# Experts of at most 64 tokens with their high and low parts side by side, in pairs, and weights split 2048 columns at a time

## The chip, the core and the metric

One core of a Trainium2 chip. A time is the device time of one execution of the whole program, in microseconds (us). Beside the times there is a profile of one execution, with a record for each instruction of the engines: TensorE (PE, with its weight loads, PEld), VectorE (DVE), ScalarE (ACT), GpSimd (POOL), and of the queues that issue DMAs (SPq is the sync engine's).

## What is computed

One decoder layer on 512 tokens of 1024 values. Its first part (norms, two kinds of attention, an output projection) is not touched. The second part is a mixture of 32 experts, of which each token takes four:

```python
logits = jnp.dot(xf, w_router) + b_router            # top 4 of 32, softmax over the four
def expert_block(args):
    xb, eb = args
    up = jnp.dot(xb, w_up[eb]) + b_up[eb]            # 1024 x 2048
    glu, lin = jnp.split(up, 2, axis=-1)
    glu = jnp.minimum(glu, 7.0)
    lin = jnp.clip(lin, -7.0, 7.0)
    act = glu * jax.nn.sigmoid(1.702 * glu) * (lin + 1.0)
    return jnp.dot(act, w_down[eb]) + b_down[eb]     # 1024 x 1024
```

The output of a token is the sum of its four experts' rows, weighted with the softmax, then normed and added to the token. With these inputs the 30 experts that are sorted by their tokens (experts 0 and 1 are not) have 169, 122, 118, 112, 107, 106, 99, 81, 80, 78, 77, 75, 71, 70, 63, 62 and then 54 to 13 tokens.

## The kernel before

All values are float32. To multiply them at nearly that precision, an operand is split into a high part (rounded to the matmul's fp32r, on ScalarE) and a low part (the rest, on VectorE); a product is then high by high, high by low and low by high, three matmuls that add up in PSUM.

The tokens of one expert are gathered into slots, on partitions. A step handles 128 slots (or 256). KINDS names the 21 steps: nine S (one expert, 128 slots), eight T (two experts, 96 and 32 slots), three P (two experts, 64 slots each) and one X (one expert, 256 slots); experts with many tokens are put, by a rank that the program works out, where there are many slots. For each expert w_up is read in eight blocks of 128 x 2048 and w_down in four of 256 rows, which also are 128 x 2048 in memory: twelve weights of 1.05 MB each. The loads go through the sync engine's queue into NW = 10 raw buffers (rawtile), each issued as its buffer comes free. wsplit (L1089) makes high and low parts, in two halves of 1024 columns each, out of NH = 8 and NL = 5 buffers; both instructions are recorded at L111. mm_w (L1128) multiplies: the slots' transposed activations are the stationary operand, the weight is the moving one, 512 columns at a time. Each block of 512 columns takes three matmuls: high x by high w (L1131), high x by low w (L1132), low x by high w (L1134). In steps T and P the second expert goes first, over all slots up to its end, and the first one then starts its slots anew, so that both share the PSUM tiles ug, ul (up) and dn (down); a matmul has 64, 96 or 128 stationary columns. A bias is added by a matmul of the rows bt with a column of ones (mm_b, L1140).

In a step the order of the listing is: up of this step's experts, two weights of the previous step's down split ahead (NA), the transposes of the next step's tokens (tsplit, L1119), the activation (act_part, L1163: two clips on VectorE, a sigmoid on ScalarE, a product on GpSimd at L1167, a last product on VectorE), then the previous step's down, its copy out of PSUM (ScalarE, L1226) and its scatter to memory (GpSimd's queue, L1217), and the transposes of the activation. The listing's order isn't the order on an engine: a planner with a cost model of its own chooses, ahead of the run, in which order each engine issues what is ready by the model; each engine then keeps that order and waits where it must.

The last expert's result goes into the sum over each token's rows without a scatter (from L1464 on). After it stands a loop for tokens past their expert's slots (from L1504 on), which has nothing to do with these counts, in either form of the kernel.

Of the kernel before, what the change touches and what calls it, by code (L numbers as in the profile page):

```python
# [9 lines left out]
F32 = mybir.dt.float32  # L10
# [20 lines left out]
NW = 10  # L31
NH = 8
NL = 5

# The slots of the experts of a step: S and X one expert, the others several that share 128. The first E0 steps take
# experts 0 ... E0 - 1; the others go by the number of tokens, those with most to the places with most slots. Tokens past
# the slots of an expert are left to a loop at the end.
SLOTS = {"S": (128,), "X": (256,), "P": (64, 64), "T": (96, 32)}
KINDS = "SSTTPSTPXTTSSSSTPTTSS"
# [3 lines left out]
def _steps():  # L43
    """(slots, first place) of the steps, the rank by tokens that each place takes, and the slots by rank"""
# [9 lines left out]
C_ID, C_IO, C_E, C_R, C_P0, C_J, C_KY, C_KP, C_K = 0, 128, 256, 288, 320, 321, 325, 357, 358   # kept to the end  # L54
C_TI, C_TS, C_NM, C_VR, C_N = 0, 128, 256, 384, 385                         # up to the experts
# [51 lines left out]
    # hi (ACT) and lo (DVE) float32r parts of src  # L107
# [11 lines left out]
def emit(tc, A, dbg=None, stop_at=99):  # L119
# [57 lines left out]
    # silu(c)  # L177
# [6 lines left out]
    strip = dram.tile([8, 128, 384], F32, name="strip")      # the biases of distances 255 ... -128, 128 times  # L184
    far = k.sp.tile([128, 8], F32, name="far")               # the bias of all larger distances
# [11 lines left out]
    def ada(part):  # L197
# [12 lines left out]
        # column (j, b) of this part is 32 * j of block b  # L210
# [5 lines left out]
    def rstd_of(ss, n, name):  # L216
        """1 / sqrt(ss / n + eps): a first guess from the exponent, then two steps of third order."""
# [20 lines left out]
    def rstd_ln(ss, n, name):  # L238
        """the same from ln and exp, with a Newton step."""
# [1317 lines left out]
```

## Time and profile before

| | us |
|---|---|
| median of three runs | 1755.59 |
| least and greatest of them | 1754.2, 1759.06 |
| profiled execution, first to last instruction | 1753.6 |
| TensorE busy in it | 1634.2 |
| VectorE busy | 1409.0 |
| ScalarE busy | 1085.6 |
| GpSimd busy | 202.9 |

The profiled execution's span is 2 us under the median. A matmul's end is modelled in the trace, and successive ones overlap: its pace is read from the starts. The share of busy time is an average over a first part of some 449 us, the experts, and the end.

### The profile page before, as it was taken

To read this page: it belongs to the slowest core of one execution; us is meant where nothing else is said; L and a number is where in the kernel's file an instruction comes from. 1 tells how busy PE (TensorE), PEld (TensorE's weight loads), DVE (VectorE), ACT (ScalarE), POOL (GpSimd) and SP (SyncE) were. 2 spreads that over 40 slices of the span, in tenths; PEclk is the share of its full clock that TensorE was granted. 3 is DMA by queue.
4 is the path that set the end of the run, shared out by engine and by line. 5 is a ranking of instruction groups with operands and counts; after the bars stand their busy time and mean duration, and the time that the engine had idled before them with its cause. 6 is when DMAs were issued, how large, how long until landed. Compare 5 with 4: busy or idle time off the path is not lost.

```text
span 1753.6 us, 22917 instructions
## 1 busy us (share of the span) xinstructions
PE 1634.2 (93%) x7691; PEld 1205.0 (69%) x7691; DVE 1409.0 (80%) x1848; ACT 1085.6 (62%) x1373; POOL 202.9 (12%) x180
## 2 busy tenths in 40 slices
PE   6999999987799999999999999999999999999980
PEld 2878765766577777777767777777777767677760
DVE  2885657768898898897985887899997888888877
ACT  3554445654667777766665666777776668576741
POOL 0200201003510110010101101011110100000002
PEclk9999999996799999999999999999999999999995
DMA  8522264085779899898886798899899989898842
GB/s 280 158 72 73 82 249 175 25 281 236 267 296 365 341 339 398 344 344 346 327 323 251 293 360 295 324 354 365 336 357 369 350 316 371 304 361 321 329 192 111
DMA packets 120575, 494.42 MB, mean 282 GB/s; under 512 B 13658, under 2 KB 38723, under 8 KB 84739
## 3 DMA queue, kind: packets, MB, share of 16 engines
q1 hardware_dynamic: 112723, 472.12, 71.5%
q0 software_dynamic: 7728, 20.77, 3.5%
q8 instruction: 62, 1.02, 0.2%
q14 instruction: 62, 0.51, 0.1%
HBM read 473.45 MB, written 25.69 MB: 285 GB/s over the span
## 4 chain that ended last, share of the span: by engine, by line
PE 61%; DVE 6%; issue 1%; DMA 1%; ACT 1%; POOL 0%; DVEq 0%; ACTq 0%
PE ug L1131 6%; PE dn L1132 6%; PE ul L1131 6%; PE ug L1132 6%; PE ul L1132 6%; PE dn L1131 6%; PE ul L1134 6%; PE ug L1134 6%; PE dn L1134 6%; DVE wlo L111 3%; PE aT L1119 1%; PE dn L1140 1%; PE ug L1140 1%; DMA raw<-in_w_up_dram 1%; PE xT L1119 1%
## 5 line engine op out<-in xcount | busy, mean ns | idle before, releaser
L111 DVE TENSOR_TENSOR wlo<-raw,whi 128x1024 fp32r<-128x1024 f32 x768 | 922.8, 1251 | 101.2 <-ACT whi L111 54.9
L111 ACT ACTIVATE whi<-raw 128x1024 fp32r<-128x1024 f32 x768 | 771.7, 1053 | 235.4 <-PE ug L1134 126.9
L1132 PE MATMUL dn<-wlo,ah 128*128 128x512 f32 (+2 forms) x528 | 211.9, 401 | 12.5 <-DVE wlo L111 12.5
L1131 PE MATMUL dn<-whi,ah 128*128 128x512 f32 (+2 forms) x528 | 212.2, 402 | 3.9 <-ACT ah L111 3.9
L1131 PE MATMUL ug<-whi,xh 128*128 128x512 f32 (+2 forms) x496 | 199.3, 402 | 4.5 <-DVE g L1164 2.2
L1131 PE MATMUL ul<-whi,xh 128*128 128x512 f32 (+2 forms) x496 | 198.4, 400 | 1.8 <-ACT whi L111 1.8
L1132 PE MATMUL ug<-wlo,xh 128*128 128x512 f32 (+2 forms) x496 | 197.2, 398 | 0.1
L1132 PE MATMUL ul<-wlo,xh 128*128 128x512 f32 (+2 forms) x496 | 196.5, 396 | 0.0
L1134 PE MATMUL dn<-whi,al 128*128 128x512 f32 (+2 forms) x528 | 167.9, 398 | 0.0
L1134 PE MATMUL ug<-whi,xl 128*128 128x512 f32 (+2 forms) x496 | 156.9, 395 | 0.0
L1134 PE MATMUL ul<-whi,xl 128*128 128x512 f32 (+2 forms) x496 | 155.5, 395 | 0.0
L1167 POOL TENSOR_TENSOR l<-l,g 128x1024 f32<-128x1024 f32 (+1 forms) x22 | 64.7, 2941 | 666.8 <-DVE l L1165 499.0
L1132 PEld LDWEIGHTS dn<-wlo,ah 128*128 128x128 f32 (+2 forms) x528 | 94.0, 178 | 44.9 <-DVE wlo L111 17.7
L1131 PEld LDWEIGHTS dn<-whi,ah 128*128 128x128 f32 (+2 forms) x528 | 94.0, 178 | 37.1 <-issue 6.7
L1131 PEld LDWEIGHTS ug<-whi,xh 128*128 128x128 f32 (+2 forms) x496 | 87.7, 177 | 37.1 <-issue 5.4
L1134 PEld LDWEIGHTS dn<-whi,al 128*128 128x128 f32 (+2 forms) x528 | 93.2, 178 | 28.5
L1131 PEld LDWEIGHTS ul<-whi,xh 128*128 128x128 f32 (+2 forms) x496 | 87.6, 177 | 30.4 <-ACT whi L111 4.5
L1132 PEld LDWEIGHTS ul<-wlo,xh 128*128 128x128 f32 (+2 forms) x496 | 87.4, 176 | 29.9 <-issue 1.9
L1132 PEld LDWEIGHTS ug<-wlo,xh 128*128 128x128 f32 (+2 forms) x496 | 87.8, 177 | 27.6 <-DVE wlo L111 2.0
L1134 PEld LDWEIGHTS ug<-whi,xl 128*128 128x128 f32 (+2 forms) x496 | 87.5, 177 | 28.0 <-DVE xl L111 0.4
L1134 PEld LDWEIGHTS ul<-whi,xl 128*128 128x128 f32 (+2 forms) x496 | 87.3, 176 | 27.8
L1217 POOL DMA_INDIRECT y<-g,dis x22 | 28.2, 1280 | 284.3 <-ACT g L1226 283.9
(520 smaller groups left out, 2345.7 us busy)
## 6 DMA issues: line engine op xcount, KB each, us to landing
raw<-in_w_up_dram SPq DMA_DIRECT2D x247, 1024.0 KB, 6.9
raw<-in_w_down_dram SPq DMA_DIRECT2D x128, 1024.0 KB, 7.3
wada<-in_w_ada_dram SPq DMA_DIRECT2D x24, 1024.0 KB, 6.7
y<-zero SPq DMA_DIRECT2D x4, 2048.0 KB, 14.3
raw<-in_w_up_dram SPq DMA_DIRECT2D x16, 512.0 KB, 6.8
raw<-y SPq DMA_DIRECT2D x7, 1024.0 KB, 9.0
wor<-in_w_out_dram SPq DMA_DIRECT2D x4, 1024.0 KB, 5.5
x<-in_x_dram SPq DMA_DIRECT2D x8, 256.0 KB, 5.8
```

Of the source, the lines that this page charges most:

```text
L111: return (nc.scalar.activation(hi, src, AF.Copy), nc.vector.tensor_sub(lo, src, hi.bitcast(F32)))
L1119: nc.tensor.transpose(pz[:, kk, :], src[:, kk * 128:(kk + 1) * 128], ident)
L1131: nc.tensor.matmul(o[0:r], lhsT=xT[0][:, kk, 0:r], rhs=wh, start=first, stop=False)
L1132: nc.tensor.matmul(o[0:r], lhsT=xT[0][:, kk, 0:r], rhs=wl, start=False, stop=False)
L1134: nc.tensor.matmul(o[0:r], lhsT=xT[1][:, kk, 0:r], rhs=wh, start=False, stop=False)
L1140: nc.tensor.matmul(o[0:r], lhsT=sel_[h].to_broadcast([64, r]), rhs=bt[h, c:c + 512], start=False, stop=True)
L1167: nc.gpsimd.tensor_tensor(l, l, g, op=OP.mult)
L1217: st = nc.gpsimd.indirect_dma_start(out=y4, out_offset=bass.IndirectOffsetOnAxis(ap=di, axis=0), in_=ys, in_offset=None, bounds_check=S * ...
```

## The change

- KINDS has 24 steps: fifteen S, one X and eight H. H has two experts of at most 64 tokens. tsplit puts, for each expert of an H, the high parts of its 64 slots and then the low parts next to each other, so that 128 stationary columns hold both. mm_w then takes two matmuls for each 512 columns (that operand by high w, and by low w) instead of three; PSUM partitions 0 to 63 hold the products of the high parts, 64 to 127 those of the low parts. T and P are gone.
- To add the two halves of an H, mm_c copies partitions 64 to 127 of PSUM into bt (ScalarE, two copies of 1024 columns for up, one for down), and a matmul with cm (the bias selector above an identity, written by GpSimd for each pair) adds them and the bias to partitions 0 to 63. Each expert of an H has an activation (act_part) and a copy out of its own, on 64 partitions; the last product (act_end) and the scatter are common to the pair.
- wsplit splits 2048 columns with one instruction on each engine, with three buffers of 2048 for the high and three for the low parts; the raw buffers are nine.
- The activation has no product on GpSimd: VectorE clips and multiplies in one instruction that reads PSUM, and clips the sigmoid with the last product.
- up and down are generators that the loop interleaves: an H's two ups each with a piece of the previous step's down behind it; after an H, each half of an S's up is followed by the down of one of the two experts.
- In mm_w the order of the matmuls of other steps is high by high, low by high, high by low. Bias rows lie in a [128, 3072] tile on 64 partitions for all columns.

The core of the diff:

```diff
-NW = 10
-NH = 8
-NL = 5
+NW = 9
+NH = 3
+NL = 3
+SG7 = 1.0 / (1.0 + math.exp(-1.702 * 7.0))
-SLOTS = {"S": (128,), "X": (256,), "P": (64, 64), "T": (96, 32)}
-KINDS = "SSTTPSTPXTTSSSSTPTTSS"
+SLOTS = {"S": (128,), "X": (256,), "H": (64, 64)}
+KINDS = "SSHHXHSSHSSHSSSHSSSHSSHS"
...
     def wsplit(raw):
-        for h in range(2):
-            hi, lo = (wp.tile([128, 1024], F32R, name=f"w{t}{h}{nb[0]}", tag=t, bufs=n) for t, n in (("hi", NH), ("lo", NL)))
-            k.split(hi, lo, f[:, h * 1024:(h + 1) * 1024])
+        hi, lo = (wp.tile([128, 2048], F32R, name=f"w{t}{nb[0]}", tag=t, bufs=n) for t, n in (("hi", NH), ("lo", NL)))
+        k.split(hi, lo, f)
...
     tsplit:
+        t = ep.tile([128, 8, 256], F32R, name=f"{nm}t{nb[0]}", tag=f"t{s_}")
+        w = kd[0] if len(kd) > 1 else 128
+        v = t.rearrange("p k (e c s) -> p (k e) c s", c=2, s=w)
+        return t, k.split(v[:, :, 0], v[:, :, 1], pz.rearrange("p k (e s) -> p (k e) s", s=w)), s_
...
+    def mm_w(outs, xT, kk, ws, first, j=None, last=False):
+        if j is not None:
+            x = xT[0][:, kk, 128 * j:128 * j + 128]
+            for c in range(2):
+                for o, w in zip(outs, ws):
+                    nc.tensor.matmul(o, lhsT=x, rhs=w[c], start=first and c == 0, stop=last and c == 1)
+            return
...
+    def mm_c(ps_, cm, c0):
+        for n, pt in enumerate(ps_):
+            nc.scalar.activation(bt[64:128, c0 + 1024 * n:c0 + 1024 * n + 1024], pt[64:128].rearrange("p a n -> p (a n)"),
+                                 AF.Copy)
+        for n, pt in enumerate(ps_):
+            for h in range(2):
+                c = c0 + 1024 * n + 512 * h
+                nc.tensor.matmul(pt[0:64, h], lhsT=cm, rhs=bt[:, c:c + 512], start=False, stop=True, skip_group_check=True)
...
-    def act_part(pg_, pl_, g, l, sg, mid=None):
-        nc.vector.tensor_scalar(g, pg_, 7.0, None, op0=OP.min)
+    def act_part(pg_, pl_, l, sg):
         nc.vector.tensor_scalar(l, pl_, 8.0, -6.0, op0=OP.min, op1=OP.max)
-        nc.scalar.activation(sg, g, AF.Sigmoid, scale=1.702)
-        nc.gpsimd.tensor_tensor(l, l, g, op=OP.mult)
-        if mid:
-            mid()
-        nc.vector.tensor_tensor(l, l, sg, op=OP.mult)
+        nc.scalar.activation(sg, pg_, AF.Sigmoid, scale=1.702)
+        nc.vector.scalar_tensor_tensor(l, pg_, 7.0, l, op0=OP.min, op1=OP.mult)
+    def act_end(l, sg):
+        nc.vector.scalar_tensor_tensor(l, sg, SG7, l, op0=OP.min, op1=OP.mult)
...
     down_gen, after the last of four weights:
+        for py in pys:
+            if j is None:
+                mm_b([py[:, 0], py[:, 1]], sel_, (2048, 2560))
+            else:
+                mm_c((py,), sel_, 2048)
...
     the loop over the steps:
+        if pair:
+            nc.gpsimd.tensor_copy(cm[0:64], sel[:, 1, e:e + 2][:, :, None].to_broadcast([64, 2, 64]))
+                ups = [(up_gen(xT, wus[j], sel_[j], lambda pg_, pl_, o=slice(64 * j, 64 * j + 64): act_part(
+                    pg_[0:64], pl_[0:64], l[0][o], sg[o]), j), 8) for j in range(2)]
+            dns = [(0, 4), (1, 4)] if pn == "H" else [(0, 4)] if pn == "X" or len(ups) == 1 else [(0, 2), (0, 2)]
+        if len(ups) < len(dns):
+            ups = [(ups[0][0], 4), (ups[0][0], 4)]
+        for n, (g_, c) in enumerate(ups):
+            for _ in range(c):
+                fin = next(g_)
+            if n < len(dns):
+                pd.ahead(dns[n][0], NA)
...
+            if fin:
+                fin()
+            if last and not two:
+                act_end(l[0], sg)
+            if n < len(dns):
+                pd.run(*dns[n])
```

## Rows read from the trace of the kernel before

**Rows 1.** The busy time of each stretch (columns: stretch, its length, then busy us and instruction count of PE, weight loads, DVE, ACT, POOL, then granted TensorE clock, share of the DMA engines and GB/s): all that lies ahead of the experts, the experts' weights, and the end.

```profile
0.00:449.30 449.30, 398.27 (x2211) 299.31 (x2212) 299.05 (x787) 221.13 (x500) 52.85 (x100) 0.94 0.48 165
449.30:1676.00 1226.70, 1204.81 (x5355) 883.28 (x5356) 1049.67 (x980) 838.69 (x844) 134.32 (x73) 0.99 0.88 333
...
1686.00:1753.60 67.60, 22.72 (x89) 15.98 (x87) 50.29 (x76) 19.54 (x24) 12.43 (x6) 0.70 0.42 167
```

**Rows 2.** The waits of the experts' stage: TensorE's longest, the loads' queue (SPq) and ScalarE's (who waited for whom, us in total, times, longest).

```profile
PE dn L1132 <- DVE wlo L111: 10.8, 8, 1.6
...
SPq L945 <- DVE wlo L111: 521.6, 192, 9.8
...
ACT whi L111 <- PE ug L1134: 126.9, 159, 2.1
```

**Rows 3.** The page's groups of matmuls (line, engine, operation, output<-operands, shapes, count, busy us and mean ns, idle before); each output has as many in L1132 and in L1134, and ul has as many as ug.

```profile
L1131 PE MATMUL dn<-whi,ah 128*128 128x512 f32 (+2 forms) x528 | 212.2, 402 | 3.9 <-ACT ah L111 3.9
L1131 PE MATMUL ug<-whi,xh 128*128 128x512 f32 (+2 forms) x496 | 199.3, 402 | 4.5 <-DVE g L1164 2.2
...
L1131 PE MATMUL u<-whi,xh 128*128 128x512 f32 x64 | 25.5, 399 | 0.5 <-DVE sg L1165 0.4
```

**Rows 4.** The timeline of TensorE at the start of two weights that follow each other in the fifth step, whose experts have 64 slots (twelve matmuls lie between the starts), and at the step's transposes (start, us, engine, line, operation).

```profile
702.98 0.40 PE L1131 MATMUL ug<-whi,xh 128*64 128x512 f32 x1
...
705.75 0.40 PE L1131 MATMUL ug<-whi,xh 128*64 128x512 f32 x1
...
709.45 1.09 PE L1119 MATMUL xT<-cst,xg 128*128 128x128 f32 x8
```

**Rows 5.** The timeline of GpSimd, only its product of each step's activation (L1167): its starts mark the steps. The second step (511.55), two steps T (1049.33, 1122.18), three steps S (1223.07 to 1297.78), the last step.

```profile
511.55 2.37 POOL L1167 TENSOR_TENSOR l<-l,g 128x1024 f32<-128x1024 f32 x1 [22.75 <-DVE l L1165]
...
1049.33 2.77 POOL L1167 TENSOR_TENSOR l<-l,g 128x1024 f32<-128x1024 f32 x1 [47.95 <-DVE tis L1072]
...
1122.18 2.42 POOL L1167 TENSOR_TENSOR l<-l,g 128x1024 f32<-128x1024 f32 x1 [42.91 <-DVE l L1165]
...
1223.07 3.33 POOL L1167 TENSOR_TENSOR l<-l,g 128x1024 f32<-128x1024 f32 x1 [23.28 <-DVE l L1165]
...
1259.99 3.33 POOL L1167 TENSOR_TENSOR l<-l,g 128x1024 f32<-128x1024 f32 x1 [23.49 <-DVE tis L1072]
...
1297.78 3.32 POOL L1167 TENSOR_TENSOR l<-l,g 128x1024 f32<-128x1024 f32 x1 [21.06 <-DVE l L1165]
...
1678.90 3.30 POOL L1167 TENSOR_TENSOR l<-l,g 128x1024 f32<-128x1024 f32 x1 [26.16 <-DVE l L1165]
```

**Rows 6.** Groups of VectorE and ScalarE over the whole span, by shape, and one piece of VectorE's timeline in the sixth step.

```profile
L111 DVE TENSOR_TENSOR wlo<-raw,whi 128x1024 fp32r<-128x1024 f32 x768 | 922.8, 1251 | 101.2 <-ACT whi L111 54.9 <-PE ug L1132 13.3 <-PE u L1132 12.3
...
L1164 DVE TENSOR_SCALAR g<-ug 128x1024 f32<-128x1024 f32 x20 | 24.5, 1223 | 20.7 <-PE ul L1140 19.9
...
L111 DVE TENSOR_TENSOR wol<-wor,woh 128x2048 fp32r<-128x2048 f32 x4 | 9.2, 2289 | 4.0 <-ACT woh L111 4.0
...
L111 ACT ACTIVATE whi<-raw 128x1024 fp32r<-128x1024 f32 x768 | 771.7, 1053 | 235.4 <-PE ug L1134 126.9 <-PE dn L1134 57.8 <-PE u L1134 15.5
...
L111 ACT ACTIVATE woh<-wor 128x2048 fp32r<-128x2048 f32 x4 | 7.7, 1913 | 0.7 <-PE y L95 0.5
...
719.66 9.35 DVE L111 TENSOR_TENSOR wlo<-raw,whi 128x1024 fp32r<-128x1024 f32 x8
```

**Rows 7.** VectorE's split at the time of GpSimd's product: the timeline of the last step, and the tile's durations (ns: least, median, longest).

```profile
1678.73 4.56 DVE L111 TENSOR_TENSOR wlo<-raw,whi 128x1024 fp32r<-128x1024 f32 x2
...
L111 DVE TENSOR_TENSOR wlo<-raw,whi x768: 1203/1218/3470, 441.8 to 1699.5; 128x1024 fp32r<-128x1024 f32 x192
```

**Rows 8.** Windows of the experts' stage in which the DMA engines' share was 0.99 to 1.00 (columns as in rows 1), and the page's line of the software queue, which holds the gathers and scatters.

```profile
659.00:684.00 25.00, 25.00 (x112) 19.52 (x111) 21.82 (x21) 18.49 (x19) 1.02 (x1) 1.00 1.00 409
684.00:709.00 25.00, 25.00 (x110) 14.49 (x109) 20.69 (x18) 17.10 (x18) 0.00 (x0) 1.00 1.00 379
...
1010.00:1020.00 10.00, 10.00 (x46) 8.19 (x45) 8.85 (x8) 7.05 (x8) 0.00 (x0) 1.00 0.99 351
...
q0 software_dynamic: 7728, 20.77, 3.5%
```

**Rows 9.** The end of a step on the timeline: the fifth step's last bias products, ScalarE's copy of the result and the next weight's first product; and the same at the last step.

```profile
733.69 0.70 PE L1140 MATMUL dn<-bt,sel 64*96 64x512 f32 x2
...
734.48 1.02 ACT L1226 ACTIVATE g<-dn 128x1024 f32<-128x1024 f32 x1 [1.01 <-PE dn L1140]
735.17 0.48 PE L1131 MATMUL ug<-whi,xh 128*128 128x512 f32 x1
...
1689.24 1.02 ACT L1226 ACTIVATE g<-dn 128x1024 f32<-128x1024 f32 x1 [7.05 <-PE dn L1140]
...
1691.23 0.50 PE L1131 MATMUL dn<-whi,ah 128*128 128x512 f32 x1 [1.79 <-ACT ah L111]
```

**Rows 10.** Windows around the start of the experts (columns as in rows 1), and TensorE's timeline in the first of them.

```profile
430.00:440.00 10.00, 0.92 (x19) 0.64 (x18) 9.71 (x37) 1.55 (x3) 2.50 (x2) 0.50 0.57 211
...
449.87 0.63 PE L1132 MATMUL ug<-wlo,xh 128*128 128x512 f32 x1
450.29 0.63 PE L1131 MATMUL ug<-whi,xh 128*128 128x512 f32 x1
```

More of the change, by code (lines that the diff above doesn't have):

```diff
@@ L1149, in up, with up_gen @@
+    def up_gen(xT, wsrc, sel_, act_, j=None, gate=(), between=iter(())):
         pg_, pl_ = ptile("ug", "uA"), ptile("ul", "uB")
         outs = [pg_[:, 0], pg_[:, 1], pl_[:, 0], pl_[:, 1]]
[L1151 to L1159 removed]
@@ L1390, in emit @@
         sel_ = [sel[:, int(i >= E0), x:x + 1] for x in range(e, e + len(ws_))]
-        two = kd[0] > 128
+        two, pair = kd[0] > 128, len(kd) > 1
+        if pair:
+            cm = cmb[nh % 2]
+            nh += 1
+            nc.gpsimd.tensor_copy(cm[0:64], sel[:, 1, e:e + 2][:, :, None].to_broadcast([64, 2, 64]))
+            sel_ = [cm[:, j] for j in range(2)]
         xs = [gather(ti) for ti, _ in idx[i + 1]] if i + 1 < len(steps) else []
+        kn = steps[i + 1][0] if i + 1 < len(steps) else ()
@@ L1393, in emit @@
         if two:
-            pu = up_act2(xT, wus[0], sel_)
-        elif i == 0:
-            pu = up(xT, kd, wus, sel_, (first,) + xT[2], between)
-            rank, xi, pos2, tab2 = tb
-        else:
-            pu = up(xT, kd, wus, sel_)
-        if i == 1:
-            prev = (tsplit(l[0], "a"),), *prev[1:]
-        if i + 1 >= E0 and (i + 1 - E0) % NB == 0 and i + 2 < len(steps):
-            prep(range(i + 2, min(i + 2 + NB, len(steps))))
-        if i == XS + 3:
-            selx, xrow = more(rank, xi)
@@ L1406, in emit @@
[L1406 to L1414 removed]
+            l = [etile("l"), etile("sg")]
+            g_ = up2_gen(xT, wus[0], sel_[0], l)
+            ups = [(g_, 4), (g_, 4)]
+        else:
+            l, sg = [etile("l")], etile("sg")
+            if pair:
+                ups = [(up_gen(xT, wus[j], sel_[j], lambda pg_, pl_, o=slice(64 * j, 64 * j + 64): act_part(
+                    pg_[0:64], pl_[0:64], l[0][o], sg[o]), j), 8) for j in range(2)]
+            else:
+                ups = [(up_gen(xT, wus[0], sel_[0], lambda pg_, pl_: act_part(pg_, pl_, l[0], sg),
+                               gate=((first,) + xT[1]) if i == 0 else (), between=between if i == 0 else iter(())), 8)]
@@ L1415, in emit @@
+        aTs = [tsplit(a, "a", kd) for a in l]
         if len(xs) > 1:
             nxt = [nxt, tsplit(xs[1], "x")]
-        prev = (aTs, kd, wds, sel_, [di for _, di in idx[i]], ("dn", "uA") if two else ("dn",))
+        if i + 1 < len(steps):
+            prev = (Down(aTs, kd, wds, sel_, [di for _, di in idx[i]], ("dn", "uA") if two else ("dn",)),
+                    "X" if two else "H" if pair else "S")
         xT = nxt
@@ L1479, in emit @@
     ysl = list(free)
-    (py,) = down_mm(aTs, ("dn",), kd, wds, sel_)
+    pys = []
+    for _ in down_gen(aTs, ("dn",), wds[0], sel_[0], [], pys.extend):
+        pass
+    py = pys[0]
     yq = [ytile(q) for q in range(NQ)]
@@ L1522, in emit, with out_ @@
             wu, wd = wsrc(ev, True)
-            pu = up(tsplit(gather(ti), "x"), (128,), [wu], [selc])
-            down([tsplit(act(pu), "a")], (128,), [wd], [selc], [di])
+            l, sg = etile("l"), etile("sg")
+            for fin in up_gen(tsplit(gather(ti), "x"), wu, selc[0:64], lambda pg_, pl_: act_part(pg_, pl_, l, sg)):
+                pass
+            fin()
+            act_end(l, sg)
+            def out_(pys):
+                ys = etile("y")
+                nc.scalar.activation(ys, pys[0], AF.Copy)
+                scatter(ys, di)
+            for _ in down_gen([tsplit(l, "a")], ("dn",), wd, selc[0:64], [], out_):
+                pass
         yq = [ytile(q) for q in range(NQ)]
```

210 lines of the change are left out of this document (119 added, 91 removed).

## The prediction

> **What bounds the kernel now.** First the stretches of the span: of 1753.6 us the experts' weights take 1226.7, from 449.3 to 1676.0, and the rest is hardly touched [rows 1]. In that stretch TensorE is busy 1204.8 us, VectorE 1049.7, ScalarE 838.7, and the DMA engines' share is 0.88: one engine is full and two others are near it. Then the waits: TensorE's longest item is 10.8 us, while the loads wait 522 us for VectorE's low parts to free a raw buffer and ScalarE waits 127 us for TensorE to free a high part [rows 2]. So buffers are full behind TensorE, and TensorE bounds the stage. Its work is a count times a pace. The groups give 528 + 496 + 496 + 64 products per line over three lines, 4752 matmuls [rows 3], which is 33 blocks of 128 slots by 144. Two weights of twelve matmuls start 2.77 us apart, 0.231 us per matmul, although these have 64 stationary columns [rows 4]: a narrow operand is no cheaper, so 4752 x 0.231 = 1098 of the 1205 us.
>
> **Part 1, two products in place of three.** After the change 17 blocks of 128 slots take 144 matmuls and 16 experts in H take 96: 3984. That removes 768 x 0.231 = 177 us from TensorE. The biases stay 6 per expert and block. Three more steps add 48 transposes at 1.09 per eight [rows 4], 6.5 us. On TensorE alone the stage would shrink by 170 us, to some 1055. This can't all be had, since VectorE, ScalarE and the loads still handle 384 weights, and during an H TensorE needs only 8 x 0.231 = 1.85 us for each.
>
> **Part 2, VectorE and ScalarE.** Two splits of 1024 columns one behind the other take 1.16 each, from eight in 9.35 us; a single split of 2048 took 2.29 against 1.22 for 1024, so 1.07 more, and 1.16 + 1.07 = 2.2 back to back [rows 6, 7]. 384 x (2.32 - 2.2) saves 45 us of VectorE. Activations: three VectorE operations per S as before, five per H in place of three per pair; with 24 steps instead of 21 that adds about 25 + 6 operations of 1.15 us (rows 6, the clip g, less the overlap), 36 us. VectorE's total stays about level, near 1040 us. It was never the bound over the whole stage, but in an H it comes before TensorE. ScalarE's 2048-column split takes 1.91 [rows 6], below VectorE's 2.2, and covers itself.
>
> **Part 3, the loads.** The same 403 MB must come in less time. The best 25 us at a full share moved 409 GB/s, the others 379 and 351 [rows 8]. I take 409, because the loads in the slower windows were still let in at the pace at which TensorE freed buffers (1.05 MB per 2.77 us is 379 GB/s), and keep 351 as the other bound. At 409 a weight takes 2.56 us, and a step's gather and scatter (20.8 MB in 22 pairs, about 1 MB) 2.5 us.
>
> **Part 4, the waits that are added.** mm_c puts ScalarE between TensorE's last product and the addition. A copy of 1024 columns takes 1.02 [rows 9], on half the partitions I take the same: TensorE waits 2 x 1.02 + 0.3 = 2.3 us behind each up of an H and 1.3 behind each down. Queued behind it are the transposes and the next down or up; queued behind the copies on ScalarE are the next weights' high parts, for which VectorE waits. Bounds per wait: zero, if the planner puts other products first, and the whole chain of the slower rival below. I take the plain wait.
>
> **Part 5, GpSimd.** Its product goes. When it runs, two of VectorE's splits take 4.56 us where two normally take 2.36, and the longest single one took 3.47 against a median of 1.22 [rows 7]. VectorE may win about 2.2 us per step, TensorE at most that. I leave the gain in the range.
>
> **The sum, step by step.** Take an S behind an S: twelve weights, 33.2 us, and by the marks 36.9 and 37.8 [rows 5]; the mean is 37.4, so 4.2 us beside the weights (six biases 1.4, two sets of transposes 2.2, the rest waits). By this a T or P is 24 x 2.77 + 4.2 + 1.4 = 72.1 (marks: 72.9), the X 74.3. From the second step's mark to the last one, 511.55 to 1678.90, there are eleven T and P, seven S and the X: 1129 against 1167.4 measured [rows 5], 3.4% more than the table.
>
> After, between the same two marks, each kind of step is the largest of TensorE, VectorE and loads:
> - S behind S, 7 times: 37.4, TensorE.
> - S behind H, 6: eight S weights and eight H weights, 37.0 + 4.2 + 0.5, and two down waits 2.6: 44.3 on TensorE (VectorE 16 x 2.2 + 5.8 = 41.0, loads 43.5).
> - H behind S, 6: sixteen H weights and four S weights. TensorE 40.7 + 5.1 + 4.6 = 50.4, VectorE 44 + 8.1 = 52.1, loads 20 x 2.56 + 2.5 = 53.7: 53.7.
> - H behind H, once: loads 64.0 (VectorE 60.9, TensorE 57). X behind H: TensorE 68.4. H behind X: TensorE 63.0.
>
> Together 1045. With the same 3.4%, 1080: 87 us less than 1167.4. The first split before the first product is 1.9 us longer (1.91 + 2.29 against 1.05 + 1.22). The end after the last mark is unchanged. So the span goes from 1753.6 to about 1669; the median lies 2 us over this profile's span, which gives 1671. Waits hidden and no excess give 1041 in place of 1080, or 1632; twice the excess, 1117, gives 1708.
>
> **The rivals.**
> 1. The loads bind everywhere. At 379 GB/s a weight takes 2.77: H behind S becomes 57.9, S behind H 46.8, H behind H 69.0, together 1091, with the excess 1128: 1719. At 351 without excess it is 1151 and 1742. For it: the share is already 0.99 to 1.00 in those windows. Against it: 409 for 25 us, and nine raw buffers that carry an H over from the easier S steps.
> The Trainium skill (DMA: Bandwidth & Descriptors, section Measured) gives 341 GB/s for one 1 MB transfer and 425 for 16 MB. By 341 the table would be 1181 and the time about 1769, no gain at all; the trace disagrees, with 409 GB/s in windows of 1 MB loads, several of which are in flight together.
> 2. The product on GpSimd was most of the excess, and the queues balance: the table without excess, 1632.
> 3. Slower: ScalarE stands at the copies. If the planner places the next weights' high parts behind the copies, then behind each up TensorE waits for two copies, then four biases pass, then a split on ScalarE and one on VectorE: 2.04 + 0.92 + 1.91 + 2.29 = 7.2 us; behind each down 6.7 with the copy out. 32 such places, 222 us. Forecast and before are equal when 2.7 us more than forecast are exposed at each place; at half exposure 111 us, of which 16 are in the sum: 1766. For it: in the last step ScalarE's copy out was followed by a wait of 1.79 us on TensorE. Against it: in the fifth step the copy ran at 734.48 and the next weight's product at 735.17 without an idle moment, so its parts had been made before the copy [rows 9].
> 4. Slower by the clock: TensorE has gaps in an H. It was granted half speed, 1.2 of 2.4 GHz, when it had been busy 0.9 of 10 us, and then a matmul took 0.42 [rows 10]; H weights of 3.4 us would add some 30 us to each H, about 1910. Against it: gaps here are a few us with work between, and the stage's clock was 0.99 [rows 1].
> The Trainium skill (TensorE: Matmul & The Clock Gate, section HAM oscillation) tells of a kernel that fell back to the low clock in every gap between loads; no row of this stage shows that.
> 5. It doesn't do what it says: with another bound throughout, the 177 us on TensorE buy nothing, 1756.
>
> **How the numbers follow.** Forecast 0.62, rival 1 0.13, rival 2 0.12, rival 3 0.08, rival 4 0.02, rival 5 0.03. Faster by over 0.3% (5 us, about what a measurement of this kernel can tell): 0.62 + 0.13 + 0.12 = 0.87; same 0.03; slower 0.10. The range runs from the table without excess, 1630, into rival 1, to 1725, and leaves out its far end and rivals 3 to 5.
>
> **What would show it.** Right: TensorE's products fall to 3984 at 0.231; VectorE's splits take 2.2; S behind S keeps its 37 us; H behind S takes 52 to 56 with the loads near 400 GB/s; TensorE idle some 5 us in an H. Wrong: waits of TensorE for a ScalarE copy (bt) of over 3 us each; ScalarE or VectorE waiting for raw over tens of us; a granted clock below 0.95; splits much longer than 2.3.

## The result, and the profile after

| | before | after |
|---|---|---|
| median of four runs, us | 1757.32 | 1707.3 |
| least and greatest | 1754.2, 1764.1 | 1704.95, 1708.33 |
| profiled execution, first to last instruction | 1753.6 | 1706.5 |

The ratio is 0.9715, with a 95% interval from 0.9691 to 0.9739: 50 us or 2.9% faster. The forecast was 1671, so 36 us of the gain that it counted on are missing; 1707 lies at the 1708 that it gave for twice the excess, but the excess sits elsewhere than the forecast put it, so the fit is chance.

The stretches of the span after (columns as in [rows 1]). Only the middle one changed much: 1190.7 us where [rows 1] has 1226.7, and the experts' stage now ends near 1640 instead of near 1680. These ends are set by hand; between the last VectorE product of the second step and that of the last step it is 1116.3 us where before has 1167.6. TensorE's busy time fell from 1205 to 1090, the clock from 0.99 to 0.97.

```profile
0.00:449.30 449.30, 402.35 (x2205) 302.20 (x2206) 297.99 (x784) 219.78 (x496) 49.76 (x92) 0.93 0.47 160
449.30:1640.00 1190.70, 1090.29 (x4690) 811.32 (x4689) 1036.71 (x646) 868.54 (x549) 102.60 (x67) 0.97 0.91 345
1640.00:1706.50 66.50, 20.55 (x80) 14.56 (x78) 48.58 (x71) 19.70 (x21) 13.25 (x6) 0.69 0.41 165
```

The groups by shape (columns as in [rows 3] and [rows 6]). The products: the eight H together have 256 in each of six groups (ug, ul, dn by the high and by the low part), the other steps 272 + 240 + 240 + 64 in each of three lines: 1536 + 2448 = 3984, as forecast. The splits are half as many and 2.29 us each; what TensorE waits for now is the low part, a wait that [rows 2] has at 10.8 us.

```profile
L113 DVE TENSOR_TENSOR wlo<-raw,whi 128x2048 fp32r<-128x2048 f32 x384 | 864.9, 2292 | 96.4 <-ACT whi L113 95.5
L113 ACT ACTIVATE whi<-raw 128x2048 fp32r<-128x2048 f32 x384 | 718.8, 1911 | 143.7 <-PE dn L1143 39.7 <-PE ul L1143 24.2 <-PE ug L1143 20.2
L1137 PE MATMUL ug<-wlo,xt 128*128 128x512 f32 x256 | 91.5, 439 | 26.5 <-DVE wlo L113 22.5
L1145 PE MATMUL dn<-wlo,at 128*128 128x512 f32 x272 | 88.2, 406 | 15.0 <-DVE wlo L113 15.0
...
L1145 PE MATMUL ug<-wlo,xt 128*128 128x512 f32 x240 | 79.2, 410 | 1.3 <-DVE wlo L113 0.8
...
L1145 PE MATMUL u<-wlo,xt 128*128 128x512 f32 x64 | 20.2, 397 | 0.0
```

TensorE's waits in the stage (who waited for whom, us in total, times, longest). The forecast's own addition, the wait for ScalarE's copy (bt), is a few us in sixteen experts; the low parts come first, and then three single waits of 6 to 7 us (the one for xg, gathered tokens, lies ahead of the second step's mark).

```profile
PE dn L1137 <- DVE wlo L113: 24.2, 20, 2.7
PE ug L1137 <- DVE wlo L113: 22.5, 24, 4.3
PE dn L1145 <- DVE wlo L113: 15.0, 20, 1.0
PE ug L1137 <- ACT y L1263: 7.2, 1, 7.2
PE xT L1120 <- DMA xg<-h2d,tis: 7.1, 1, 7.1
PE xrow L1388 <- DVE xtab L1377: 6.4, 1, 6.4
...
PE ug L1160 <- ACT bt L1155: 2.8, 4, 1.9
```

GpSimd's product is gone, so the last VectorE product of a step's activation (act_end, L1190) marks the steps. Its starts, the marks from here on, cut the stage into steps; these are the windows between marks of six of them (columns as in [rows 1]): an H behind an H, the X with the H behind it, the H of the ninth step, and late ones, an H behind an S, an S behind an H, an S behind an S.

```profile
591.07:648.95 57.88, 47.03 (x198) 32.80 (x196) 55.33 (x37) 48.13 (x32) 1.02 (x1) 0.97 1.00 378
648.95:801.68 152.73, 138.14 (x588) 104.96 (x589) 111.09 (x69) 94.37 (x63) 12.59 (x9) 0.96 0.80 296
...
870.09:949.39 79.30, 67.21 (x276) 50.59 (x275) 69.86 (x70) 56.37 (x36) 5.97 (x4) 0.91 0.87 340
...
1390.20:1452.17 61.97, 56.81 (x239) 39.64 (x240) 57.90 (x34) 48.70 (x32) 6.53 (x3) 1.00 0.99 379
1452.17:1495.55 43.38, 38.66 (x166) 28.62 (x165) 37.03 (x20) 32.88 (x21) 1.43 (x1) 1.00 0.94 355
1495.55:1533.92 38.37, 36.79 (x164) 28.10 (x164) 33.30 (x24) 26.67 (x17) 4.59 (x2) 1.00 0.92 340
```

Against the forecast's table, from the second step's mark (519.43) to the last (1635.71):

| step | times | table, us | measured mean | difference in all |
|---|---|---|---|---|
| S behind S | 7 | 37.4 | 36.5 | -6 |
| S behind H | 6 | 44.3 | 41.4 | -17 |
| H behind S | 6 | 53.7 | 66.9 (the last three 62.5, 62.0, 61.0) | +79 |
| H behind H | 1 | 64.0 | 57.9 | -6 |
| X, and H behind X | 1 | 131.4 | 152.7 | +21 |
| together | | 1045 | 1116 | +71 |

The table had been given 35 us of excess all over; it needed 71, and they are in two kinds of step. Singles came out at the table or below it.

**Why an H takes 62.** TensorE's timeline in the second up projection of the H that ends at 1452 (first instruction on the low part of each weight; eight matmuls lie between two such lines). A weight starts every 2.20 us, where its eight matmuls take 8 x 0.233 = 1.86 (1426.75 to 1427.22 is two of them, 0.47). TensorE is hardly idle by the list of waits, because each matmul's modelled end hides the gap; the starts show it.

```profile
1426.18 0.73 PE L1137 MATMUL ug<-wlo,xt 128*128 128x512 f32 x2 [0.29 <-DVE wlo L113]
1426.75 0.63 PE L1137 MATMUL ul<-wlo,xt 128*128 128x512 f32 x2
1427.22 0.63 PE L1137 MATMUL ug<-whi,xt 128*128 128x512 f32 x2
...
1428.38 0.72 PE L1137 MATMUL ug<-wlo,xt 128*128 128x512 f32 x2
...
1430.59 0.73 PE L1137 MATMUL ug<-wlo,xt 128*128 128x512 f32 x2
...
1432.79 0.73 PE L1137 MATMUL ug<-wlo,xt 128*128 128x512 f32 x2
```

VectorE's timeline in the same place: nine splits in 19.89 us, 2.21 each, without a gap. That is the pace of TensorE above. At the end of each up its clip of PSUM then stands 1.40 us, and TensorE's next low part with it.

```profile
1419.38 1.22 DVE L1184 TENSOR_SCALAR l<-ul 64x1024 f32<-64x1024 f32 x1 [1.40 <-PE ul L1160]
...
1423.85 19.89 DVE L113 TENSOR_TENSOR wlo<-raw,whi 128x2048 fp32r<-128x2048 f32 x9
1445.14 1.22 DVE L1184 TENSOR_SCALAR l<-ul 64x1024 f32<-64x1024 f32 x1 [1.40 <-PE ul L1160]
```

What the queue of the loads waits for in this H (1390 to 1452; columns as in [rows 2]): for 42 of 62 us a load can't be issued because VectorE has not yet let go of a raw buffer. In the whole stage no split waits for a load to land.

```profile
SPq L947 <- DVE wlo L113: 24.2, 12, 4.3
SPq L118 <- DVE wlo L113: 17.8, 8, 4.3
```

**Where the X loses.** ScalarE's and TensorE's timeline behind the 256-token step (776 to 782). The step copies two down results out; there is one buffer y, so the second copy stood 5.09 us until the first scatter had left it, the splits of the next H stood behind the copy on ScalarE, and TensorE stood 7.23. Then its matmuls ran 0.43 us apart (4 in 1.71, 778.34 to 780.05), which is the rate at 1.2 GHz [rows 10]; the granted clock was 0.50 from 777.3 to 781.8, and the first window below has 0.71 with the faster rest in it.

```profile
776.25 1.02 ACT L1263 ACTIVATE y<-dn 128x1024 f32<-128x1024 f32 x1 [5.09 <-DMA y<-y,dis]
777.33 1.22 PE L1137 MATMUL ug<-whi,xt 128*128 128x512 f32 x2 [7.23 <-ACT y L1263]
778.34 1.05 PE L1137 MATMUL ug<-wlo,xt 128*128 128x512 f32 x2
...
780.05 1.05 PE L1137 MATMUL ug<-wlo,xt 128*128 128x512 f32 x2
```

**The ninth step** (79.3 us where later ones of its kind take 62) holds the work that prepares the extra rounds (more, some forty small VectorE instructions and three row transposes). ScalarE stood 8.6 us there for the transposed tokens, TensorE 6.4 us for the table; of 880 to 895 TensorE was busy a third. The windows of both places, the X's and this one (columns as in [rows 1]):

```profile
777.30:785.00 7.70, 7.67 (x24) 5.93 (x24) 4.48 (x3) 6.42 (x4) 1.00 (x1) 0.71 0.19 46
...
880.00:895.00 15.00, 5.24 (x20) 4.19 (x21) 8.49 (x34) 3.04 (x4) 3.02 (x2) 0.64 0.78 298
895.00:909.00 14.00, 14.00 (x57) 11.12 (x56) 11.58 (x6) 12.60 (x8) 0.00 (x0) 0.90 0.52 194
```

**The first H** (71.6 us) has a wait of the same sort. VectorE had to stand until a scatter let go of the indices that it was to write anew (dis); TensorE then stood 4.31 us for a low part, and from 544.2 to 549.0 its clock was 0.50. VectorE's timeline:

```profile
541.79 0.17 DVE L1076 SCALAR_TENSOR_TENSOR dis<-tis,svs 128x3 int32<-128x3 int32 x1 [5.10 <-DMA y<-y,dis]
```

### The profile page after: what moved, and what is told of

The parts are those of the page before. It is cut to its first block, busy times and chain, and to the rows that moved or that the text cites. A ratio compares the mean times of both kernels' runs of the same rounds, so it can differ in the third digit from the quotient of the medians.

```text
span 1706.5 us, 19861 instructions
## 1 busy us (share of the span) xinstructions
PE 1513.2 (89%) x6971; PEld 1128.1 (66%) x6971; DVE 1383.3 (81%) x1499; ACT 1108.0 (65%) x1066; POOL 165.6 (10%) x164
## 5 line engine op out<-in xcount | busy, mean ns | idle before, releaser
L113 DVE TENSOR_TENSOR wlo<-raw,whi 128x2048 fp32r<-128x2048 f32 x384 | 864.9, 2292 | 96.4 <-ACT whi L113 95.5
L113 ACT ACTIVATE whi<-raw 128x2048 fp32r<-128x2048 f32 x384 | 718.8, 1911 | 143.7 <-PE dn L1143 39.7
L1137 PE MATMUL ug<-wlo,xt 128*128 128x512 f32 x256 | 91.5, 439 | 26.5 <-DVE wlo L113 22.5
L1137 PE MATMUL dn<-wlo,at 128*128 128x512 f32 x256 | 87.4, 424 | 24.5 <-DVE wlo L113 24.2
L1145 PE MATMUL dn<-wlo,at 128*128 128x512 f32 x272 | 88.2, 406 | 15.0 <-DVE wlo L113 15.0
L1137 PE MATMUL ug<-whi,xt 128*128 128x512 f32 x256 | 84.2, 409 | 7.2 <-ACT y L1263 7.2
L1141 PE MATMUL dn<-whi,at 128*128 128x512 f32 x272 | 87.8, 401 | 1.8 <-ACT y L1268 1.8
L1143 PE MATMUL dn<-whi,at 128*128 128x512 f32 x272 | 86.9, 397 | 0.0
L1137 PE MATMUL dn<-whi,at 128*128 128x512 f32 x256 | 84.6, 411 | 1.9 <-ACT whi L113 1.9
L1137 PEld LDWEIGHTS ug<-wlo,xt 128*128 128x128 f32 x256 | 42.8, 194 | 63.6 <-DVE wlo L113 59.0
L1141 PE MATMUL ul<-whi,xt 128*128 128x512 f32 x240 | 78.0, 406 | 4.9 <-DVE l L1184 4.9
L1137 PE MATMUL ul<-wlo,xt 128*128 128x512 f32 x256 | 81.8, 401 | 0.4 <-DVE wlo L113 0.4
L1137 PE MATMUL ul<-whi,xt 128*128 128x512 f32 x256 | 81.2, 398 | 0.0
L1145 PE MATMUL ug<-wlo,xt 128*128 128x512 f32 x240 | 79.2, 410 | 1.3 <-DVE wlo L113 0.8
L1143 PE MATMUL ul<-whi,xt 128*128 128x512 f32 x240 | 77.2, 403 | 2.0 <-DVE xt L113 2.0
L1141 PE MATMUL ug<-whi,xt 128*128 128x512 f32 x240 | 77.2, 402 | 1.2 <-issue 1.2
L1143 PE MATMUL ug<-whi,xt 128*128 128x512 f32 x240 | 77.9, 400 | 0.0
L1145 PE MATMUL ul<-wlo,xt 128*128 128x512 f32 x240 | 77.2, 399 | 0.0
L1137 PEld LDWEIGHTS dn<-wlo,at 128*128 128x128 f32 x256 | 47.1, 196 | 44.2 <-DVE wlo L113 35.6
L1145 PEld LDWEIGHTS dn<-wlo,at 128*128 128x128 f32 x272 | 49.3, 189 | 33.8 <-DVE wlo L113 23.7
L1106 POOL DMA_INDIRECT xg<-h2d,tis x25 | 50.6, 2023 | 211.0 <-PE xT L1120 127.6
```

What stands on the lines that cost most here:

```text
L113: return (nc.scalar.activation(hi, src, AF.Copy), nc.vector.tensor_sub(lo, src, hi.bitcast(F32)))
L1106: k.last = nc.gpsimd.indirect_dma_start(out=t, out_offset=None, in_=h2d, in_offset=bass.IndirectOffsetOnAxis(ap=ti, axis=0), bounds_check= ...
L1137: nc.tensor.matmul(o, lhsT=x, rhs=w[c], start=first and c == 0, stop=last and c == 1)
L1141: nc.tensor.matmul(o, lhsT=xh, rhs=wh, start=first, stop=False)
L1143: nc.tensor.matmul(o, lhsT=xl, rhs=wh, start=False, stop=False)
L1145: nc.tensor.matmul(o, lhsT=xh, rhs=wl, start=False, stop=False)
```

## The experiments

The theory after the result (V): VectorE's low parts set the length of the paired steps. The rivals: the loads do (L), ScalarE's copies do (C), the shape of the steps around the X and the extra rounds does (P). Each kernel was timed in three rounds against the kernel before, which took 1755.1 to 1757.0 in these comparisons; "after" is 1707.3. The last column is the time from the first step's mark to the last one in the profiled execution (before 1193.4, after 1144.8). Most of these edits touch nothing ahead of the first mark, yet it lies anywhere from 484.6 to 493.2 in those runs; so a difference of a few us is read from this column too.

| label | median, us | ratio to before | interval | mark to mark, us |
|---|---|---|---|---|
| e1_nolo | 1633.4 | 0.9296 | 0.9273 to 0.9319 | 1069.7 |
| e2_noadd | 1704.4 | 0.9708 | 0.9689 to 0.9727 | 1142.2 |
| e3_split1024 | 1709.1 | 0.9728 | 0.9711 to 0.9744 | 1149.5 |
| e4_xs | 1706.8 | 0.9713 | 0.9686 to 0.9739 | 1144.3 |
| e5_y2 | 1700.8 | 0.968 | 0.9661 to 0.9699 | 1139.1 |
| e6_more | 1702.7 | 0.9697 | 0.9681 to 0.9713 | 1140.0 |
| e7_before_act | 1746.8 | 0.9938 | 0.9921 to 0.9954 | 1187.6 |
| e8_before_split2048 | 1783.2 | 1.016 | 1.0139 to 1.0181 | 1219.3 |
| e9_y2_more | 1693.9 | 0.9642 | 0.9626 to 0.9658 | 1132.1 |
| e10_y2_more_hi4 | 1692.3 | 0.9634 | 0.9618 to 0.9651 | 1130.2 |
| e11_no_pairs | 1799.9 | 1.0239 | 1.0222 to 1.0256 | 1236.9 |
| e12_nolo_one | 1702.4 | 0.9698 | 0.9682 to 0.9714 | 1141.7 |

### No low parts in the pairs

```diff
 wsplit(raw, j):                       # j: an expert of an H
+        if j is not None:
+            nc.scalar.activation(hi, f, AF.Copy)
+            return [(hi[:, n * 512:(n + 1) * 512],) * 2 for n in range(4)]
...
 the calls of wsplit: pass the expert's place in its pair, or None
```

> The changed kernel, but the weights of the pairs H have no low part on VectorE: TensorE uses the high part twice, so the low-weight term of those experts is left out of the result. 192 of the 384 low splits go, some 192 x 2.2 = 422 us of VectorE, all of it in or behind the H steps; TensorE's products and the loads stay. Theory V (an H is bound by VectorE, in the profile 57.9 of 62 us busy): the H steps fall from 62 to 52 to 54 us, where loads or TensorE bind, in all 50 to 70 us, about 1645. Theory L (the loads bind an H at some 380 GB/s with a full DMA share): the H steps stay at 58 to 62, the whole between 1690 and 1707. Theory P (single places: the step behind X, the step with the table of further blocks): no more than 15 us.

74 us below after. The windows of a late H behind an S and of the S behind it (columns as in [rows 1]):

```profile
1328.88:1388.30 59.42, 56.12 (x251) 42.60 (x252) 25.23 (x19) 51.41 (x33) 3.01 (x3) 1.00 0.98 391
1388.30:1425.55 37.25, 35.70 (x158) 27.19 (x157) 21.72 (x14) 27.63 (x19) 1.41 (x1) 1.00 1.01 405
```

VectorE went from 57.9 to 25.2 us and the two steps from 105.4 to 96.7, with the same loads. So the loads did not hold the steps at 105, although their share was 0.99 then: L falls. The forecast's table has 53.7 + 44.3 = 98.0 for these two steps, so without the low parts they are no longer over it. The H alone came only to 59.4, not to the 52 to 54 expected under V. ScalarE was busy 51.4 us of it, and none of its splits waited for a load; what holds it there isn't shown.

### No copies and no addition of the halves

```diff
 mm_c:
-            nc.scalar.activation(bt[64:128, ...], pt[64:128]..., AF.Copy)
-                nc.tensor.matmul(pt[0:64, h], lhsT=cm, rhs=bt[:, c:c + 512], ...)
+                nc.tensor.matmul(pt[0:64, h], lhsT=cm[0:64], rhs=bt[0:64, c:c + 512], ...)
```

> The changed kernel without the addition of the two halves of an H: no copies of PSUM partitions 64 to 127 by ScalarE, and the bias matmul works on 64 rows; the products of the low parts of the activations of the H experts are left out of the result. Theory V with waits (ScalarE stands 3 us in front of each copy and VectorE and TensorE then wait for the next high part): 16 ups at 1.4 to 2.5 and 16 downs at up to 1, some 30 us, about 1677. Theory L or P: no change, 1700 to 1707.

3 us below after, within its uncertainty; a late H takes 61.1 to 62.6 as in after. C falls. VectorE's clips, which stood 1.40 us each in the late H of after, stand 0.15 here, but VectorE now stands 3.1 us for high parts in that step, where it stood 0.6.

### Halves of 1024 columns again

```diff
-NH = 3
-NL = 3
+NH = 6
+NL = 6
 wsplit: for h in range(2): hi, lo of 1024 columns; k.split(hi, lo, f[:, h * 1024:(h + 1) * 1024])
```

> The changed kernel with each weight split in two halves of 1024 columns again, six buffers each (the same memory). A pair of halves costs VectorE 2.32 instead of 2.2 and ScalarE 2.0 instead of 1.91. Theory V: 192 weights of the H experts by 0.12, some 20 us slower, about 1727. Theory L or P: 1707; if the finer grain lets TensorE begin earlier, 1695.

2 us above after. A late round of H, S, S, S took 66.4 + 43.2 + 38.3 + 37.6 = 185.5 us against 62.5 + 43.4 + 35.4 + 41.6 = 182.9, so the finer splits did cost where VectorE paces, by 2.6 us in four steps, while the X with its H took 144.9 instead of 152.7 and gave some of it back; mark to mark it is 4.7 us longer. The expected 20 us were wrong. Two of the waits in question are smaller here but not gone: the second copy stands 2.8 us for the first scatter, where it stood 5.1, and TensorE stands for the table at the row transposes:

```profile
PE xrow L1391 <- DVE xtab L1380: 5.7, 1, 5.7
...
PE xrow L1391 <- DVE xtab L1386: 2.9, 1, 2.9
```

### A single behind the X

```diff
-KINDS = "SSHHXHSSHSSHSSSHSSSHSSHS"
+KINDS = "SSHHXSHSHSSHSSSHSSSHSSHS"
```

> The changed kernel with the step X followed by an S instead of an H (KINDS SSHHXSHSHSS... in place of SSHHXHSSHSS...), nothing else. Theory P: behind X the down of 256 slots runs 22 us on TensorE alone while ScalarE stands behind two copies into one buffer and VectorE idles, the step took 85 us where my table had 63; with the eight weights of an S behind it instead of the second half of an H, 15 to 20 us less, about 1690. Theories V and L: the work is the same, 1700 to 1710.

No change. The X with its S took 102.8, the H behind them 82.9; the copy out stood 7.8 us for the scatter here too. It isn't the kind of step behind the X that costs.

### A second buffer for the copied down result

```diff
-                    ys = etile("y")
+                    ys = ytile()        # "y" and "y2" in turn
```

> After with a second buffer for the copied down result, used in turn by every step, so that the second copy of the 256-token expert need not wait until the first scatter has left its buffer. In after that copy waited 5.09 us, VectorE behind it 4.0 and 8.1 us, and the step took 85.3 us where the table had 63.0. If the one buffer makes that step long: the wait (5.09) and the TensorE idle behind it (7.2) go, the step comes to 73 to 78 us, the whole kernel 7 to 12 us below after. If the lone down projection of the 256-token expert (22 us of TensorE beside 10.6 of 25 us of VectorE) is the cause and the buffer only lies under it: the wait goes and the step stays within 3 us, the time within 3 us of after.

6.5 us below after (the intervals of the two ratios still touch), and the trace has it in the expected place: the X with its H takes 143.8 instead of 152.7. ScalarE's timeline there: both copies run in one go, the next splits behind them.

```profile
763.39 1.92 ACT L1269 ACTIVATE y<-dn 128x1024 f32<-128x1024 f32 x2
766.35 9.13 ACT L113 ACTIVATE whi<-raw 128x2048 fp32r<-128x2048 f32 x5 [1.04 <-PE ug L1137]
```

### The extra rounds prepared later

```diff
-                if i == XS + 3:
+                if i == XS + 9:
```

> After with the work that sets up the extra rounds (some 40 small VectorE instructions, three transposes) six steps later, in a step that follows a single and is followed by a single, where loads set the pace. In after it stood in a step of 79.3 us where a step of its kind takes 62, with ScalarE waiting 8.6 us for VectorE's results and TensorE 6.4 us at the row transposes. If its place is what costs, since the paired step before it left VectorE behind: 8 to 12 us below after. If the work costs the same wherever it stands: within 3 us of after, with the TensorE wait at the row transposes in the new place.

4.6 us below after (here too the intervals overlap). The ninth step takes 60.7 instead of 79.3; some of that went to its neighbours, which had been short because the ninth step had let their weights run ahead (34.1 to 38.3 and 38.3 to 44.6). The size lies between the two expectations.

### Before with the new activation alone

```diff
-        nc.vector.tensor_scalar(g, pg_, 7.0, None, op0=OP.min)
-        nc.gpsimd.tensor_tensor(l, l, g, op=OP.mult)
+        nc.vector.scalar_tensor_tensor(l, pg_, 7.0, l, op0=OP.min, op1=OP.mult)
...
 the sigmoid reads PSUM; its clip goes into the last product
```

> Before with the new activation alone: the clamps inside the two products, no product on GpSimd; all steps, splits and buffers as before. By the second rival (GpSimd's product made VectorE's splits slow, and that was most of the excess over the table): 15 to 35 us below before. By the forecast's account (TensorE bound the old steps and the splits were hidden): within 6 us of before.

10 us below before, 5.8 mark to mark: between the two. VectorE's splits were a little shorter without GpSimd's product (1221 ns, where [rows 6] has 1251, over 768 of them 23 us), and at most half of that reached the end. The edit also takes a link out of the activation's chain, for which VectorE stood 8.7 us in all in before (its last products, waiting for GpSimd's); the run doesn't tell the two apart. By either, the second rival was a part of the excess, not most of it.

```profile
L112 DVE TENSOR_TENSOR wlo<-raw,whi 128x1024 fp32r<-128x1024 f32 x768 | 901.9, 1221 | 124.7 <-ACT whi L112 67.5 <-PE u L1133 17.8 <-PE ug L1133 14.0
```

### Before with splits of 2048 columns alone

```diff
-NH = 8
-NL = 5
+NH = 3
+NL = 3
 wsplit: one hi, lo of 2048 columns instead of two of 1024
```

> Before with weight splits of 2048 columns (three buffers of each part in place of eight and five) and nothing else. TensorE bound the old steps, so the shorter VectorE total (some 130 us less) should be hidden: within 6 us of before. If the fixed cost of each split stood on the path: 15 to 40 us below before. If the coarser grain holds up the first matmuls of a weight: 10 to 30 us above before.

26 us above before, although VectorE had less to do. 20 of them are in two steps, the T behind the X and the S in which the extra rounds are prepared (81.0 instead of 71.8 us, 63.6 instead of 52.3). The waits of those two stretches:

```profile
ACT g L1223 <- DMA y<-g,dis: 7.6, 1, 7.6
...
PE ug L1128 <- ACT g L1223: 5.3, 1, 5.3
...
PE xrow L1330 <- DVE xtab L1325: 3.2, 1, 3.2
```

In before, TensorE's weight load waited 0.3 us for the copy out in the same step. So the places at which after loses at the X and at the extra rounds came with this edit, not with the pairs. The edit has two parts, the coarse splits and the buffers: three high ones of 2048 columns hold less than eight of 1024. The run with halves of 1024 columns again, but six buffers, still has both waits, so the grain alone isn't shown to be the cause.

### Both waits out together

Both edits: ytile in place of etile("y"), and

```diff
-                if i == XS + 3:
+                if i == XS + 9:
```

> After with both: a second buffer for the copied down result (alone 1700.8, 6.5 us below after) and the setting up of the extra rounds six steps later (alone 1702.7, 4.6 us below). If the two waits are separate places, the gains add: 1696, between 1693 and 1699. If the weight buffers that are then full simply run into the next bound (VectorE in the paired steps), the second one brings nothing: 1700 to 1703.

1693.9: 13.4 us below after, where the two alone gave 6.5 and 4.6. They add; the interval lies wholly under that of after. This kernel beats both.

### Four high buffers, eight raw

```diff
-NW = 9
-NH = 3
+NW = 8
+NH = 4
```

> As the one before, with four buffers of 2048 columns for the high parts instead of three, and eight raw buffers instead of nine to make room. Before with 2048 columns and three buffers of each part was 26 us slower than before with eight and five buffers of half that size, with waits of TensorE for a copy out and for the row transposes that did not stand there before; so the theory is that the split weights between VectorE and TensorE are what covers such waits, and that three are too few. By it: 5 to 15 us below the run with three. If the raw buffers cover as much as the high ones, or if low parts are what is short (VectorE makes them last): within 4 us of it.

1692.3, 1.6 us below the last one, with the late steps as they were (62.0, 43.4, 38.4, 61.0). By this, three high buffers are not what makes the late H long. Why the coarse splits cost before 26 us isn't settled by this: with two counts changed at once, one gain may have met one loss.

### After without pairs

```diff
-KINDS = "SSHHXHSSHSSHSSSHSSSHSSHS"
+KINDS = "SSSSXSSSSSSSSSSSSSSSSSSSSSSSSSSS"
```

> After with KINDS of 31 steps of one expert each (the fifth has 256 slots) and no pair: every product takes three matmuls again, 4752 as in before, with the new splits and activation. This undoes the operand of high and low parts side by side. By the forecast's step table (37.4 us for a single behind a single, 74.3 for the 256-token step) the stretch between the second and the last mark is 29 x 37.4 + 74 = 1159, against 1116 in after; with the shortfall of a few per cent of before and the coarser splits 1190 to 1220: 1780 to 1810 for the whole. If the pairs bring little, because an expert of few tokens costs its twelve weights on VectorE either way: 1700 to 1740.

1799.9: the pairs are worth 93 us to after. From the second mark to the last it takes 1209, the table 1159 with 4.3% on top. Of the 43 us above before, the activation alone would give -10 and the splits alone +26; the rest, if these add, goes with the 32 steps in place of 21.

### One low part in twelve left out

```diff
-                w = wsplit(ahead.pop(0) if ahead else up_w(wsrc, kk))
+                w = wsplit(ahead.pop(0) if ahead else up_w(wsrc, kk), j if kk == 3 else None)
...
 wsplit as in the first run
```

> After, where one of the twelve weights of each expert in a pair (the fourth of its up projection) has no low part made; the high part is multiplied in its place, so TensorE does the same number of matmuls, and a pair loses two VectorE splits (4.4 us) and nothing else. The same as the first of these runs in a dose of one twelfth. If VectorE's total sets the length of the paired steps, as a sum over the step: each of them loses 4.4 us until it meets the 56 us at which the run without any low part stopped, so the steady ones come from 62 to 57.6 and eight of them make 25 to 35 us. If low parts only hurt at certain places of the step (the start, the turn from one expert to the other), and the loads fill the rest: 0 to 8 us.

4.9 us below after (the intervals overlap), 3.1 mark to mark, so V as a sum over the step falls: sixteen low parts less, 35 us of VectorE, gave 3 to 5. In the H that ends at 1445 VectorE is busy 4 us less than in the late H of after, and the step is 0.9 us shorter:

```profile
1383.60:1444.69 61.09, 55.55 (x239) 39.83 (x240) 53.95 (x33) 48.45 (x32) 4.98 (x3) 1.00 0.98 379
```

VectorE's timeline, and ScalarE's, in the second up of this H:

```profile
1417.75 11.21 DVE L113 TENSOR_TENSOR wlo<-raw,whi 128x2048 fp32r<-128x2048 f32 x5
1429.57 6.70 DVE L113 TENSOR_TENSOR wlo<-raw,whi 128x2048 fp32r<-128x2048 f32 x3 [0.62 <-ACT whi L113]
```

```profile
1422.53 3.90 ACT L113 ACTIVATE whi<-raw 128x2048 fp32r<-128x2048 f32 x2
1427.62 5.53 ACT L113 ACTIVATE whi<-raw 128x2048 fp32r<-128x2048 f32 x3 [1.19 <-PE ul L1142]
```

Past the gap, VectorE stood for a high part, which ScalarE made late because it had no high buffer free until TensorE was done with one. From clip to clip this up shrank from 25.8 us (1419.38 to 1445.14 in after) to 24.4, not by 2.2. The pace of 2.2 is VectorE's, but ScalarE's high parts stand right behind it: the price of a low part in a pair was 4.9 / 16 = 0.3 us here (0.2 by the marks) and 74 / 192 = 0.4 in the first run, of 2.2 us of VectorE's time.

## Why the prediction was right, and where 36 us went

- **What bounded before, and part 1: right.** 3984 products at 0.233 us. TensorE's busy time in the stage fell by 115 us where 170 were forecast: with modelled ends that hide gaps of 0.34 us a weight it can't show all of it. Without the pairs the kernel is slower than before (1799.9): they carry the whole gain.
- **Part 2: right on the split** (2.21 us back to back, 2.2 forecast), **wrong on where it counts.** The table took the H behind an S at 53.7 from the loads and put VectorE at 52.1, for 20 weights. From mark to mark it makes 22: the next S's first two are split ahead, and the S behind the H makes 14. That is 4.4 us more; the rest of its work came to 9.5 instead of 8.1, and it stands 4.0 us, 2.8 of them at the two clips. 52.1 + 4.4 + 1.4 + 4.0 = 61.9, the measured 62. The S behind it doesn't get the 4.4 back, since there TensorE sets the pace (43.4, forecast 44.3). This is the mis-sized term: 8.3 us a step, 50 in the six. The sum counts what VectorE did in that time; it doesn't say that VectorE alone holds the step, and the run without one low part in twelve says otherwise. What the run without any low parts shows is that all of them together make the excess of a late H and the S behind it.
- **Part 3: the bound was never reached.** In the late H the loads wait 42 us for VectorE to free raw buffers, while their share reads 0.99 at 379 GB/s: a full share, on which the forecast's 53.7 and rival 1 rested, was no sign of a bound. Rival 1's H behind S of 57.9 lies nearer to the measured 62 than the forecast's 53.7, but not for its reason. In the first experiment the same loads came at 391 and 405 in those steps. ([rows 2] understates this wait in before: its 521.6 us are of 600 to 1700 and of one of the two lines that issue loads; from 449.3 to 1676 both lines wait 930 us for low parts.) The Trainium skill (DMA: Bandwidth & Descriptors, section Measured) gives 341 GB/s for a single 1 MB transfer; the windows here, with loads of that size, show 379 to 405.
- **Part 4: forecast 2.3 us a wait, a few us in all were paid.** TensorE's waits for bt are 0.2 to 1.9 us; without the copies the time changes by 3 us. Rival 3 falls. What the copies cost is at VectorE's clips, 1.40 us each, and the run without them didn't win that back either: VectorE stood for high parts instead.
- **Part 5:** 6 to 10 us on the kernel before, inside the range left for it; rival 2 is a part, as far as it is GpSimd at all.
- **Not foreseen:** two places at which a stall that had been covered stood open: the single buffer y behind the X, and the preparation of the extra rounds. Together 13.4 us by experiment. Neither is in the diff's core, and in before no row shows them; the change of wsplit and its buffers uncovered them. The first H's 5.10 us for the indices (2.77 in before) is a third such wait; it still stands in the run that removes the other two (5.27).
- **Rival 4: not as put.** In the late H, whose weights start 0.34 us later than their matmuls need, the clock is 1.00. It fell behind the open waits: 0.71 in 777.3 to 785, 0.64 in 880 to 895. The Trainium skill (TensorE: Matmul & The Clock Gate, section HAM oscillation) has a kernel that falls back in every wait for a load; these two places agree with it in that a long wait came first (7.23 and 6.4 us), while the late pairs, with no long wait, are no such case.
- Of the 71 us over the table, 50 are the H behind an S at its late 62, 29 the three early ones above that (71.6, 79.3, 65.2; the second of them holds the extra rounds, the first the wait for the indices, whose price no run shows), 21 the X and its H; singles and the H behind an H gave 29 back. 35 of the 71 had been allowed for. The range, 1630 to 1725, held partly by luck: its upper end was drawn into rival 1, loads that bind everywhere (1719), and that isn't what happened.
- **Of the signs it named,** the 3984 products, splits of 2.2 us and an S behind S of 37 (36.5) came. H behind S at 52 to 56 with the loads near 400 GB/s did not (62 late, 379). None of the wrong signs came either: waits for bt of at most 1.9 us, no split waiting for raw, a clock of 0.97 in the stage.

**Open:** why splits of 2048 columns with their buffers cost the kernel before 26 us when going back to halves of 1024 costs after 2 to 5; grain and buffers weren't varied one at a time. What holds the H once VectorE is relieved, ScalarE's work, its order or the number of high buffers, is open too (more buffers and fewer low parts in one kernel wasn't tried).

## What to carry to other kernels

Count an engine's work between the marks that are compared, not by the step that its results belong to: splits made ahead moved 4.4 us into the step that had least room. When an edit takes time out of the bounding engine, the others come close to it (in the late H VectorE is busy 57.9 us of 62, TensorE 56.8 by its modelled ends, ScalarE 48.7); here no one of them alone set the time, and taking work from one gave back a fraction (0.2 to 0.4 us for 2.2). And when the cover of a stall is thinned, look for resources that occur once, such as one buffer between a copy and its scatter; a second one of 4 KB a partition gave 6.5 us.

## Not expected of the hardware

- A share of 0.99 of the DMA engines was no bound: 379 GB/s at 0.99 in an H of after, 391 at 0.98 in the same step with VectorE relieved, and 405 at 1.01 in the next.
- A wait of 7.23 us on TensorE cost more than itself: the matmuls behind it ran 0.43 us apart for 4.4 us (777.33 to 781.76), at a granted clock of 0.50. Behind the 4.31 us in the first H it was 0.50 too, from 544.2 to 549.0.
- 64 stationary columns for the high parts and 64 for the low ones run at the pace of 128 of one kind, 0.233 us per 512 columns, as [rows 4] had it for 64 alone.
